# A two-layer hybrid encoder: the first gate placed in the opening's written order, queries transposed in float32 two heads at a time, and the splits behind the transposes given the heads' priority

## The chip, the cores and the metric

One core of one Trainium2 chip runs the whole program in one launch. The time is device microseconds (us) of an execution, and a version's time is the median of several executions. A core has five engines that run side by side, each with its own queue of instructions in a fixed order: TensorE (PE: matmuls and transposes, with weight loads shown apart as PEld), VectorE (DVE), ScalarE (ACT), GpSimd (POOL) and SyncE (SP, here the queue that starts the weight transfers). An engine stops at the head of its queue until the semaphores that this instruction waits for are set; everything queued behind it waits too.

## The reference

Two layers of an encoder over 256 tokens of width 1024, in float32. Each layer has a half-step SwiGLU network, a mixing stage of two attention branches on one joint projection, and a second SwiGLU network:

```python
for l in range(DEPTH):
    x = x + 0.5 * swiglu(rms_norm(x, ffn1_norm[l]), ffn1_w_gate[l], ffn1_w_up[l], ffn1_w_down[l])
    h = rms_norm(x, mix_norm[l])
    z = h @ w_in[l]
    qa, ka, va, qs, ks_, vs, zg = jnp.split(z, splits, axis=-1)
    # 8 heads of 64 for qa, ka, va and qs; 2 shared heads for ks_, vs; q and k RMS-normed per head
    o_na = neighbourhood_attention(qa, ka, va, na_rpb[l])
    o_sw = sliding_window_gqa(qs, ks_, vs, t5_bias, sw_sink[l])
    g = jax.nn.sigmoid((zg + b_gate[l]).astype(jnp.float32))
    merged = g[:, :, 0] * (o_na @ w_branch_na[l]) + g[:, :, 1] * (o_sw @ w_branch_sw[l])
    x = x + merged @ w_out[l]
    x = x + 0.5 * swiglu(rms_norm(x, ffn2_norm[l]), ffn2_w_gate[l], ffn2_w_up[l], ffn2_w_down[l])

def swiglu(x, w_gate, w_up, w_down):
    return (jax.nn.silu(x @ w_gate) * (x @ w_up)) @ w_down
```

## The kernel before

**Products in three parts.** Every float32 operand of a large product is split in two f32r numbers, a high part (ACT copies it, `split_to` at L184) and a low part (DVE subtracts, L185). A product is then three matmuls: high by high (L170), low weights by high data (L171), high weights by low data (L172). Weights come in pieces of 256 rows by 512 columns: a transfer on SP's queue into one of 4 buffers `raw` (L142), then two tiles `wh` and `wl` in a ring of 6. A piece's next transfer can start when the `wl` subtract that last read its `raw` buffer is done.

**Tokens** are two tiles of 128 (`T` = 2). `project(t, pieces, n)` makes 24 matmuls for a token tile and one chunk of 512 columns into one of two PSUM tiles `g`; the `g` tile is free again when what reads it is done.

**What sets the order.** PE's order is that of the program. Work that comes later is put off with `defer(lag, key, fn)`, the lag counted in units of projection time, and `tick` runs what is due. For the other engines a scheduler puts the instructions in an order by priorities; code under `high_priority(500)` (the wrapper `urgent`, before the change around the steps of an attention head: `front`, `turn`, `back`) is put ahead of other work of its time. In the opening the order of ACT and DVE is written out instead: `linked(engine, emit)` (L124) ties an instruction behind the last one that was linked on this engine, as long as the dictionary `chain` is not empty.

**The opening** (L225, first chunk of the first layer's network). It makes the norm of both token tiles in halves, and the first chunk's four pieces in between (`pieces`), with `steps(t, i)` the six matmuls of token tile `t` and piece `i` (L237). Then come `square(t, half)` (ACT's sums of squares, L217, with the statistics `ms` on DVE, L221 and L222, and `rsqrt` on POOL), and the loads and splits of the second chunk (`second`: four pieces), all on the written order. After `opening` returns, the loop of `ffn` emits for each token tile the gate: `sg` = Silu on ACT (L453) and `hh` on DVE (L454), which reads the other half of the same `g` tile.

**The mixing stage** (`mix`, L477) projects in the order Q0 Q1 K0 K1 q1 q0 and so on (Q and K are queries and keys of the sliding-window branch for token tiles 0 and 1, q and k those of the neighbourhood branch, a and g values and gates). `normed` makes the normed `qn` or `kn` of a token tile: `z` and `sq` on ACT, `hv` on DVE, `rs_y` on POOL, then the product on DVE (L489). `queries` then splits `qn` into `qs` (per head 64 columns high, 64 low), and its turn transposes the eight heads one by one, four to each PSUM tile `tp` (two buffers), with ACT copying each `tp` into `qT` or `sqT` (L504): a head's 64 high rows and 64 low rows stand on the 128 partitions. `keys` doubles `kn` on POOL (L511) and transposes it in float32 (L519); ACT makes the high part, DVE the low one (`skT` in the sliding-window branch, `kh` and `kl` in the other, L521 and L522). A score `sc` (L558) is two matmuls for a query tile, with the stacked queries against high and low keys; `S`, `pt`, `ph`, `pl` and `po` are the steps of softmax and the product with the values.

Of the kernel before, what the change touches and what calls it, by code (L numbers as in the profile page):

```python
# [11 lines left out]
F32 = mybir.dt.float32  # L12
F32R = mybir.dt.float32r
# [3 lines left out]
ALU = mybir.AluOpType  # L17
# [41 lines left out]
def hybrid_encoder(ctx, tc, x, w_gu1, w_d1, w_in, b_gate, qk_gain, rpb, sink, t5,  # L59
# [30 lines left out]
    ident_r = const.tile([P, P], F32R, name="ident_r")  # L90
    nc.vector.tensor_copy(ident_r, ident)
# [133 lines left out]
    def opening(w, l):  # L225
# [35 lines left out]
        second = [piece(i, 1) for i in range(2)]  # L261
        square(1, 0, idle)
        square(1, 1, idle)
        second += [piece(i, 1) for i in range(2, KD // 2)]
        chain.clear()
        for i in (1, 2, 3):
            for t in range(T):
                steps(t, i)
# [39 lines left out]
    def ffn(l, n, w_gu, w_d, after):  # L308
        with tc.tile_pool(name="ffn", bufs=1) as fp:
# [126 lines left out]

            waiting = []
            for c in range(NFC):
                first = n == 0 and c == 0
                if first:  # L440
# [8 lines left out]
                pair = act.tile([P, T, FC], F32, name="hh", tag="xg", bufs=2)  # L449
                for t in range(T):  # L450
                    ps = both[t] if first else project(t, pieces, 512)
                    sg = fp.tile([P, FC], F32, name="sg", tag="sg", bufs=2)
                    nc.scalar.activation(sg, ps[:, :FC], AF.Silu, scale=rstd[t])  # L453
                    nc.vector.scalar_tensor_tensor(pair[:, t], ps[:, FC:], rstd[t], sg, op0=ALU.mult, op1=ALU.mult)  # L454
                waiting.append((c, pair))
# [21 lines left out]
    def mix(l, n, after):  # L477
        with tc.tile_pool(name="mix", bufs=1) as mp:
# [12 lines left out]

            def queries(key, ps, t, qT):
                qn = act.tile([P, NH, DH], F32, name="qn", tag="xg", bufs=2)
                normed(ps, t, NH, qn)
                qs = mp.tile([P, NH, 2, DH], F32R, name="qs", tag="qk", bufs=2)
                split_to(qs[:, :, 0, :], qs[:, :, 1, :], qn)

                def turn():
                    for half in range(2):
                        tp = ps_tp.tile([P, 4, P], F32R, name="tp", tag="tp")  # L500
                        for j in range(4):
                            nc.tensor.transpose(tp[:, j, :], qs[:, 4 * half + j].rearrange("p two d -> p (two d)"),
                                                ident_r)
                        nc.scalar.activation(qT[:, 4 * half:4 * half + 4, t * P:(t + 1) * P], flipped(tp), AF.Copy)  # L504

                defer(QK_LAG + MORE.get(key, 0), key, turn)

            def keys(key, ps, t, nh, g, kh, kl):
# [4 lines left out]

                def turn():
# [16 lines left out]
            def attend(name, ins, qT, kh, kl, kidx, bias_of, vcol, ready, oT, sink_l=None):  # L531
# [5 lines left out]
                def urgent(fn):  # L537
                    def run(*args):
                        with tc.high_priority(500):
                            fn(*args)  # L540
                    return run

                @urgent
                def front(h):
# [11 lines left out]
                    for t in range(T):  # L556
                        for i, k in enumerate((kh, kl)):
                            nc.tensor.matmul(ps[:, t, :], qT[:, h, t * P:(t + 1) * P], k[:, kidx(h), :],  # L558
# [50 lines left out]
            sqT = mp.tile([P, NH, S], F32R, name="sqT", tag="sq")  # L609
            skT = pair("skT", "sk", [2, S])  # L610
            sv = mp.tile([P, T, 2, 3 * DH], F32R, name="sv")
            qT = mp.tile([P, NH, S], F32R, name="qT")
# [222 lines left out]
```

## Time and profile before

| | us |
|---|---|
| median of 3 executions | 1078.03 (1077.65 to 1078.95) |
| the profiled execution's own time | 1077.96 |
| its span in the trace | 1076.2 |
| PE, DVE, ACT, POOL busy | 1069.2, 875.9, 671.6, 116.9 |
| `wl` from `raw` (DVE L185), 336 times | 404.6 |
| `wh` from `raw` (ACT L184), 336 times | 346.7 |
| projections on PE (`g`, L170 to L172), 2928 matmuls | 1139.0 in overlapping spans |

An execution takes longer than its span in the trace by the 1.8 us around it. The granted TensorE clock is 1.0 throughout. Matmuls are pipelined: a 128x512 matmul is busy 0.39 us in its row, but the next one starts 0.23 us after it, so sums of PE's rows count the overlap twice. The mixing stage of the first layer lies at about 195 to 350 us, that of the second 532 us later.

### The profile page before, as it was taken

What the parts mean: (1) busy time and instruction counts of PE and PEld (TensorE: products, weight loads), DVE (VectorE), ACT (ScalarE), POOL (GpSimd) and SP (SyncE); (2) the same over time, 40 slices, a digit from 0 to 9 for tenths busy, and PEclk for the clock granted to TensorE, in tenths of its full rate; (3) what the DMA queues carried; (4) which work ended last, traced back from release to release, by engine and by line L of the source; (5) the groups of instructions that cost most, each with busy time, mean ns of one, the idle gap of its engine ahead of it and who ended that gap; (6) DMA issues with size and microseconds to landing.
All of it is one profiled execution on the core that took longest, in us unless ns stands there. A gap on an engine that the chain in (4) does not pass through costs nothing.

```text
span 1076.2 us, 14744 instructions
## 1 busy us (share of the span) xinstructions
PE 1069.2 (99%) x5125; PEld 890.2 (83%) x5125; DVE 875.9 (81%) x1337; ACT 671.6 (62%) x1014; POOL 116.9 (11%) x118
## 2 busy tenths in 40 slices
PE   9999999999999999999999999999999999999998
PEld 6888888888888888888878888888888888888887
DVE  5688898889886768879877888988898867778795
ACT  6565754788764556565465665557877646566562
POOL 1000030243520000000000000003534000000000
PEclk9999999999999999999999999999999999999999
DMA  8667665765654667756657766648666555776562
GB/s 259 214 217 237 211 206 176 227 199 151 195 184 137 202 201 241 244 167 193 208 160 232 235 210 206 183 150 242 181 196 180 181 173 161 236 232 204 197 196 78
DMA packets 98828, 212.63 MB, mean 198 GB/s; under 512 B 7569, under 2 KB 13745, under 8 KB 98753
## 3 DMA queue, kind: packets, MB, share of 16 engines
q1 hardware_dynamic: 98560, 211.60, 62.4%
q8 instruction: 40, 0.66, 0.2%
q14 instruction: 36, 0.29, 0.1%
q0 software_dynamic: 192, 0.08, 0.1%
HBM read 210.59 MB, written 1.06 MB: 197 GB/s over the span
## 4 chain that ended last, share of the span: by engine, by line
PE 95%; DVE 2%; ACT 1%; issue 1%; DMA 0%
PE g L170 22%; PE g L172 22%; PE g L171 22%; PE acc L170 5%; PE acc L172 5%; PE acc L171 5%; PE tp L318 2%; PE sc L558 1%; PE po L593 1%; PE tp L170 1%; PE tp L172 1%; PE pt L579 1%; PE tp L171 1%; DVE wl L185 1%; PE tp L201 1%
## 5 line engine op out<-in xcount | busy, mean ns | idle before, releaser
L185 DVE TENSOR_TENSOR wl<-raw,wh 128x1024 fp32r<-128x1024 f32 x336 | 404.6, 1217 | 67.8 <-ACT wh L184 65.2
L184 ACT ACTIVATE wh<-raw 128x1024 fp32r<-128x1024 f32 x336 | 346.7, 1045 | 129.4 <-DMA raw<-in_w_gu 47.8
L170 PE MATMUL g<-wh,xh 128*128 128x512 f32 (+1 forms) x976 | 383.8, 393 | 0.8 <-DVE hh L454 0.8
L172 PE MATMUL g<-wh,xl 128*128 128x512 f32 (+1 forms) x976 | 377.8, 387 | 0.7 <-DVE xl L185 0.7
L171 PE MATMUL g<-wl,xh 128*128 128x512 f32 (+1 forms) x976 | 377.4, 387 | 0.0
L172 PEld LDWEIGHTS g<-wh,xl 128*128 128x128 f32 x976 | 183.4, 188 | 40.0 <-DVE xl L185 2.1
L170 PEld LDWEIGHTS g<-wh,xh 128*128 128x128 f32 x976 | 183.6, 188 | 33.9 <-DVE hh L454 1.2
L171 PEld LDWEIGHTS g<-wl,xh 128*128 128x128 f32 x976 | 183.7, 188 | 32.7
L453 ACT ACTIVATE sg<-g,rs_y 128x256 f32<-128x256 f32 x88 | 41.0, 466 | 91.1 <-PE g L172 78.7
L454 DVE SCALAR_TENSOR_TENSOR hh<-g,rs_y,sg 128x256 f32<-128x256 f32 x88 | 42.1, 479 | 54.0 <-ACT sg L453 53.9
L170 PE MATMUL acc<-wh,hi 128*128 128x512 f32 x180 | 71.1, 395 | 0.0
L172 PE MATMUL acc<-wh,lo 128*128 128x512 f32 x180 | 70.2, 390 | 0.0
L171 PE MATMUL acc<-wl,hi 128*128 128x512 f32 x180 | 70.1, 389 | 0.0
L176 POOL TENSOR_TENSOR rs_y<-ms,mhalf 128x1 f32<-128x1 f32 x12 | 6.7, 554 | 553.5 <-DVE ms L222 545.1
L350 DVE TENSOR_TENSOR u<-raw 128x512 f32<-128x512 f32 x64 | 41.9, 685 | 15.2 <-DMA raw<-in_w_d 15.0
L184 ACT ACTIVATE corner<-raw 128x512 fp32r<-128x512 f32 x32 | 20.2, 631 | 50.1 <-DMA raw<-in_w_d 33.0
L571 POOL TENSOR_TENSOR S<-S,sm 128x512 f32<-128x512 f32 x32 | 37.1, 1160 | 65.7 <-DVE sm L570 38.3
L172 PEld LDWEIGHTS acc<-wh,lo 128*128 128x128 f32 x180 | 33.8, 188 | 7.2
L171 PEld LDWEIGHTS acc<-wl,hi 128*128 128x128 f32 x180 | 33.8, 188 | 6.8
L170 PEld LDWEIGHTS acc<-wh,hi 128*128 128x128 f32 x180 | 33.8, 188 | 6.7
L564 ACT ACTIVATE S<-S,mx 128x256 f32<-128x256 f32 x64 | 31.9, 500 | 8.0 <-DVE mx L561 7.9
L185 DVE TENSOR_TENSOR lo<-a,hi 128x896 fp32r<-128x896 f32 x32 | 33.8, 1084 | 0.5 <-ACT hi L184 0.5
(189 smaller groups left out, 1510.4 us busy)
## 6 DMA issues: line engine op xcount, KB each, us to landing
raw<-in_w_gu SPq DMA_DIRECT2D x176, 512.0 KB, 4.2
raw<-in_w_d SPq DMA_DIRECT2D x100, 512.0 KB, 4.0
raw<-in_w_in SPq DMA_DIRECT2D x64, 512.0 KB, 4.5
raw<-in_w_out SPq DMA_DIRECT2D x16, 512.0 KB, 3.6
bb<-in_b_gate SPq DMA_DIRECT2D x16, 256.0 KB, 3.6
raw<-in_w_bsw SPq DMA_DIRECT2D x8, 512.0 KB, 3.9
raw<-in_w_bna SPq DMA_DIRECT2D x8, 512.0 KB, 3.5
raw<-in_w_d SPq DMA_DIRECT2D x12, 256.0 KB, 2.6
```

The costliest lines, as they stand in the source:

```text
L170: nc.tensor.matmul(ps, xh, wh, start=first, stop=False)
L171: nc.tensor.matmul(ps, xh, wl, start=False, stop=False)
L172: nc.tensor.matmul(ps, xl, wh, start=False, stop=last)
L184: linked("act", lambda: nc.scalar.activation(hi, src, AF.Copy))
L185: linked("dve", lambda: nc.vector.tensor_tensor(lo, src, hi.bitcast(F32), ALU.subtract))
L201: nc.tensor.transpose(tp[:, i, :], xs[t][:, k * P:(k + 1) * P], ident)
L318: nc.tensor.transpose(tp[:, SLOT[t][i], :], hh[:, t, i * P:(i + 1) * P], ident)
L350: sub = lambda to, x, y: nc.vector.tensor_tensor(to, x, y, ALU.subtract)
L453: nc.scalar.activation(sg, ps[:, :FC], AF.Silu, scale=rstd[t])
L454: nc.vector.scalar_tensor_tensor(pair[:, t], ps[:, FC:], rstd[t], sg, op0=ALU.mult, op1=ALU.mult)
L564: nc.scalar.activation(S_[:, t, :], S_[:, t, :], AF.Exp, bias=mx[:, t:t + 1], scale=-1.0, accum_out=sm[:, t:t + 1])
L571: nc.gpsimd.tensor_tensor(S_, S_, sm.unsqueeze(2).to_broadcast([P, T, S]), ALU.mult)
```

## The change

Three edits go together.

**The opening.** The matmul steps of pieces 1 to 3 are written ahead of the second chunk's loads, and a new argument `early` emits token tile 0's gate between the third square and the second of the second chunk's pieces, with `linked`, so that it stands there in the written order. The gate itself becomes a function `glu(t, ps, pair)`. PE's order in the opening stays.

**The queries.** `qn` stays float32 and isn't split. Two heads stand side by side in 128 columns, so a token tile takes four float32 transposes into one `tp` tile (with `ident`; `ident_r` and its cast go). Behind the transposes, `split_to` runs twice on 64 partitions: for even heads (e = 0) and odd heads (e = 1), ACT writes the high part to the heads' own 64 partitions and DVE the low part to the other 64. `qT` and `sqT` get the parity as a dimension of its own, and the score matmuls index `qT[:, h % 2, h // 2]`. DVE's subtract waits for ACT's copy of the same parity, and ACT's second copy waits for DVE's first subtract; the `tp` tile is free after DVE's second.

**Priority.** `urgent` moves ahead of `queries` and `keys` and wraps their turns too.

```diff
@@ opening @@
-    def opening(w, l):
+    def opening(w, l, early):
...
-        second = [piece(i, 1) for i in range(2)]
+        for i in (1, 2, 3):
+            for t in range(T):
+                steps(t, i)
+        second = [piece(0, 1)]
         square(1, 0, idle)
+        early(ps[0])
+        second.append(piece(1, 1))
         square(1, 1, idle)
         second += [piece(i, 1) for i in range(2, KD // 2)]
         chain.clear()
-        for i in (1, 2, 3):
-            for t in range(T):
-                steps(t, i)
@@ ffn @@
+            def glu(t, ps, pair):
+                if t == 0:
+                    pair[0] = act.tile([P, T, FC], F32, name="hh", tag="xg", bufs=2)
+                sg = fp.tile([P, FC], F32, name="sg", tag="sg", bufs=2)
+                linked("act", lambda: nc.scalar.activation(sg, ps[:, :FC], AF.Silu, scale=rstd[t]))
+                linked("dve", lambda: nc.vector.scalar_tensor_tensor(pair[0][:, t], ps[:, FC:], rstd[t], sg,
+                                                                     op0=ALU.mult, op1=ALU.mult))
...
-                    both, second = opening(w_gu, l)
+                    both, second = opening(w_gu, l, lambda ps: glu(0, ps, pair))
...
                 for t in range(T):
-                    ps = both[t] if first else project(t, pieces, 512)
...
+                    if not first:
+                        glu(t, project(t, pieces, 512), pair)
+                    elif t:
+                        glu(t, both[t], pair)
@@ mix @@
             def queries(key, ps, t, qT):
-                qn = act.tile([P, NH, DH], F32, name="qn", tag="xg", bufs=2)
+                qn = mp.tile([P, 2, NH, DH], F32, name="qn", tag="qk", bufs=2)[:, 0]
                 normed(ps, t, NH, qn)
-                qs = mp.tile([P, NH, 2, DH], F32R, name="qs", tag="qk", bufs=2)
-                split_to(qs[:, :, 0, :], qs[:, :, 1, :], qn)
-
+
+                @urgent
                 def turn():
-                    for half in range(2):
-                        tp = ps_tp.tile([P, 4, P], F32R, name="tp", tag="tp")
-                        for j in range(4):
-                            nc.tensor.transpose(tp[:, j, :], qs[:, 4 * half + j].rearrange("p two d -> p (two d)"),
-                                                ident_r)
-                        nc.scalar.activation(qT[:, 4 * half:4 * half + 4, t * P:(t + 1) * P], flipped(tp), AF.Copy)
+                    tp = ps_tp.tile([P, 4, P], F32, name="tp", tag="tp")
+                    for j in range(4):
+                        nc.tensor.transpose(tp[:, j, :], qn[:, 2 * j:2 * j + 2].rearrange("p two d -> p (two d)"), ident)
+                    cols = slice(t * P, (t + 1) * P)
+                    for e in range(2):
+                        a, b = e * DH, (1 - e) * DH
+                        split_to(qT[a:a + DH, e, :, cols], qT[b:b + DH, e, :, cols], flipped(tp[a:a + DH]))
...
+                @urgent
                 def turn():
                     for h0 in range(0, nh, 4):
...
-                            nc.tensor.matmul(ps[:, t, :], qT[:, h, t * P:(t + 1) * P], k[:, kidx(h), :],
+                            nc.tensor.matmul(ps[:, t, :], qT[:, h % 2, h // 2, t * P:(t + 1) * P], k[:, kidx(h), :],
```

What the change moves is seen in the order of the instructions on each engine. First ACT in the opening, where `idle,ssq` are the squares (of token tile 0, then 1), `wh` the copies of the second and then the third chunk's pieces, and `sg` the gates of token tile 0 and 1. Before:

```order
L217 ACTIVATE idle,ssq<-x_80 128x512 x2
L184 ACTIVATE wh<-raw 128x1024 x2
L217 ACTIVATE idle,ssq<-x_81 128x512
L453 ACTIVATE sg<-g,rs_y 128x256
L217 ACTIVATE idle,ssq<-x_81 128x512
L184 ACTIVATE wh<-raw 128x1024 x2
L453 ACTIVATE sg<-g,rs_y 128x256
L184 ACTIVATE wh<-raw 128x1024 x2
```

With the change:

```order
L215 ACTIVATE idle,ssq<-x_80 128x512 x2
L182 ACTIVATE wh<-raw 128x1024
L215 ACTIVATE idle,ssq<-x_81 128x512
L441 ACTIVATE sg<-g,rs_y 128x256
L182 ACTIVATE wh<-raw 128x1024
L215 ACTIVATE idle,ssq<-x_81 128x512
L182 ACTIVATE wh<-raw 128x1024 x3
L441 ACTIVATE sg<-g,rs_y 128x256
```

The first `sg` passes one `wh`; the second `sg` now stands behind five `wh` and not four, the fifth being the third chunk's first piece.

Next DVE at the same place, with `hh` of token tiles 0 and 1, `ms` the statistics and `wl` the subtracts. Before:

```order
L221 TENSOR_TENSOR ms<-ssq 128x1
L222 TENSOR_SCALAR ms<-ms 128x1
L185 TENSOR_TENSOR wl<-raw,wh 128x1024 x2
L454 SCALAR_TENSOR_TENSOR hh<-g,rs_y,sg 128x256
L221 TENSOR_TENSOR ms<-ssq 128x1
L222 TENSOR_SCALAR ms<-ms 128x1
L185 TENSOR_TENSOR wl<-raw,wh 128x1024 x2
L454 SCALAR_TENSOR_TENSOR hh<-g,rs_y,sg 128x256
```

With the change:

```order
L219 TENSOR_TENSOR ms<-ssq 128x1
L220 TENSOR_SCALAR ms<-ms 128x1
L183 TENSOR_TENSOR wl<-raw,wh 128x1024
L442 SCALAR_TENSOR_TENSOR hh<-g,rs_y,sg 128x256
L183 TENSOR_TENSOR wl<-raw,wh 128x1024
L219 TENSOR_TENSOR ms<-ssq 128x1
L220 TENSOR_SCALAR ms<-ms 128x1
L183 TENSOR_TENSOR wl<-raw,wh 128x1024 x3
L442 SCALAR_TENSOR_TENSOR hh<-g,rs_y,sg 128x256
```

The first `hh` passes one `wl`; the second stands behind one `wl` more, again that of the third chunk's first piece.

Last DVE in the first layer's mixing stage, between the second query tile and the first score of the sliding-window branch. `skT` are the low halves of the two key tiles, `qn` the normed queries of the neighbourhood branch, `sqT` the new subtracts. Before:

```order
L185 TENSOR_TENSOR wl<-raw,wh 128x1024 x2
L489 TENSOR_TENSOR qn<-z,rs_y 128x512
L522 SCALAR_TENSOR_TENSOR skT<-tp,qkg,skT 128x2x128
L185 TENSOR_TENSOR wl<-raw,wh 128x1024 x2
L522 SCALAR_TENSOR_TENSOR skT<-tp,qkg,skT 128x2x128
L185 TENSOR_TENSOR qs<-qn,qs 128x8x64
L486 TENSOR_REDUCE hv<-sq 128x8
```

With the change:

```order
L183 TENSOR_TENSOR wl<-raw,wh 128x1024
L183 TENSOR_TENSOR sqT<-tp,sqT 64x4x128
L183 TENSOR_TENSOR wl<-raw,wh 128x1024
L537 SCALAR_TENSOR_TENSOR skT<-tp,qkg,skT 128x2x128
L497 TENSOR_TENSOR qn<-z,rs_y 128x512
L183 TENSOR_TENSOR wl<-raw,wh 128x1024
L183 TENSOR_TENSOR sqT<-tp,sqT 64x4x128
L183 TENSOR_TENSOR wl<-raw,wh 128x1024
L537 SCALAR_TENSOR_TENSOR skT<-tp,qkg,skT 128x2x128
L494 TENSOR_REDUCE hv<-sq 128x8
```

Two subtracts of the second query tile come in ahead of the key tiles' low halves, the first `skT` passes `qn`, and the `qs` subtract behind the second is gone. On PE nothing moves but the transposes: `MATMUL tp<-ident_r,qs 128x128 x8` becomes `MATMUL tp<-ident,qn 128x128 x4` at eight places. The transposes of the second sliding-window key tile now use the `tp` buffer of the first, and so wait for its `skT`.

More of the change, by code (lines that the diff above doesn't have):

```diff
@@ L89, in hybrid_encoder @@
     make_identity(nc, ident)
-    ident_r = const.tile([P, P], F32R, name="ident_r")
-    nc.vector.tensor_copy(ident_r, ident)
     mhalf = const.tile([P, 8], F32, name="mhalf")
@@ L439, in ffn @@
                 first = n == 0 and c == 0
+                pair = [None]
                 if first:
[L441 removed]
+                    both, second = opening(w_gu, l, lambda ps: glu(0, ps, pair))
                 elif n == 0 and c == 1:
@@ L448, in ffn @@
                     prepare(prep[c])
-                pair = act.tile([P, T, FC], F32, name="hh", tag="xg", bufs=2)
                 for t in range(T):
-                    ps = both[t] if first else project(t, pieces, 512)
[L452 to L455, printed above, removed]
+                    if not first:
+                        glu(t, project(t, pieces, 512), pair)
+                    elif t:
+                        glu(t, both[t], pair)
+                waiting.append((c, pair[0]))
                 if c % 2 or c >= NFC - 3:
@@ L490, in normed, with urgent, run @@
                                         r.unsqueeze(2).to_broadcast([P, nh, DH]), ALU.mult)
+            def urgent(fn):
+                def run(*args):
+                    with tc.high_priority(500):
+                        fn(*args)
+                return run
             def queries(key, ps, t, qT):
-                qn = act.tile([P, NH, DH], F32, name="qn", tag="xg", bufs=2)
+                qn = mp.tile([P, 2, NH, DH], F32, name="qn", tag="qk", bufs=2)[:, 0]
                 normed(ps, t, NH, qn)
-                qs = mp.tile([P, NH, 2, DH], F32R, name="qs", tag="qk", bufs=2)
-                split_to(qs[:, :, 0, :], qs[:, :, 1, :], qn)
+                @urgent
                 def turn():
-                    for half in range(2):
-                        tp = ps_tp.tile([P, 4, P], F32R, name="tp", tag="tp")
-                        for j in range(4):
-                            nc.tensor.transpose(tp[:, j, :], qs[:, 4 * half + j].rearrange("p two d -> p (two d)"),
-                                                ident_r)
-                        nc.scalar.activation(qT[:, 4 * half:4 * half + 4, t * P:(t + 1) * P], flipped(tp), AF.Copy)
+                    tp = ps_tp.tile([P, 4, P], F32, name="tp", tag="tp")
[5 more added lines that the diff above has]
+                        split_to(qT[a:a + DH, e, :, cols], qT[b:b + DH, e, :, cols], flipped(tp[a:a + DH]))
                 defer(QK_LAG + MORE.get(key, 0), key, turn)
@@ L535, in attend @@
                     bias = [bias_of(0), bias_of(1)]
[L537 to L541, printed above, removed]
                 @urgent
@@ L607, in pair @@
                 return both[:, 0], both[:, 1]
-            sqT = mp.tile([P, NH, S], F32R, name="sqT", tag="sq")
+            sqT = mp.tile([P, 2, NH // 2, S], F32R, name="sqT", tag="sq")
             skT = pair("skT", "sk", [2, S])
             sv = mp.tile([P, T, 2, 3 * DH], F32R, name="sv")
-            qT = mp.tile([P, NH, S], F32R, name="qT")
+            qT = mp.tile([P, 2, NH // 2, S], F32R, name="qT")
             kT = (mp.tile([P, NH, S], F32R, name="kh", tag="kh"), mp.tile([P, NH, S], F32R, name="kl"))
```

## The prediction

> **What bounds the kernel now.** I read the busy times first, then the chain that ended last, then what TensorE (PE) waited for in all.
>
> ```profile
> PE 1069.2 (99%) x5125; PEld 890.2 (83%) x5125; DVE 875.9 (81%) x1337; ACT 671.6 (62%) x1014; POOL 116.9 (11%) x118
> PE 95%; DVE 2%; ACT 1%; issue 1%; DMA 0%
> PE idle L120 <- DVE blank L115: 1.6, 1, 1.6
> PE g L170 <- DVE hh L454: 0.8, 1, 0.8
> PE g L172 <- DVE xl L185: 0.7, 1, 0.7
> ```
>
> PE is busy for 99% of the span and holds 95% of the chain. The last three rows are all the waits the trace names for it (total, times, longest): 3.1 us in 1076, 0.8 of them behind `hh` in the opening. So only two things shorten this kernel: PE issuing less, or that wait going. Work taken from VectorE (DVE) or ScalarE (ACT) is worth nothing, and work added there costs only where it makes PE late. The profiled execution took 1077.96 us (span 1076.2 and 1.8 around it), 0.07 under the median of 1078.03; the sum is made against it. A measurement of this kernel tells about 0.2% (2.2 us) from no change: faster is under 1075.9, slower over 1080.2.
>
> **Part 1, fewer transposes.** A token tile of queries now takes eight f32r transposes (L502); it will take four float32 ones. The trace has a batch of four with the same kind of operand, `pt` (L579).
>
> ```profile
> L502 PE MATMUL tp<-ident_r,qs 128*128 128x128 f32 x64 | 6.4, 244 | 0.0
> 208.59 0.80 PE L502 MATMUL tp<-ident_r,qs 128*128 128x128 f32 x8
> 209.22 0.46 PE L170 MATMUL g<-wh,xh 128*128 128x512 f32 x1
> 209.52 0.39 PE L171 MATMUL g<-wl,xh 128*128 128x512 f32 x1
> 233.44 0.60 PE L579 MATMUL pt<-ident,S 128*128 128x128 f32 x4
> 233.79 0.48 PE L170 MATMUL g<-wh,xh 128*128 128x512 f32 x1
> 234.10 0.40 PE L171 MATMUL g<-wl,xh 128*128 128x512 f32 x1
> ```
>
> Matmuls overlap, so a batch costs the distance between starts, not its busy time. Eight: 208.59 to 209.22 is 0.63, and the matmul behind needs 0.30 to the next. Four: 0.35, then 0.31. That is 0.93 against 0.66, 0.27 saved per batch. 64 transposes are 8 batches (two token tiles, two attention branches, two layers): **8 x 0.27 = 2.2 us**, 1.1 in each layer's attention stage. PE's other rows are unchanged.
>
> A rule would turn this term round: a float32 pass through PE as four passes. The f32r batch steps by 0.63 / 8 = 0.08; four times four of these are 1.27, so a batch would lose 0.64 and the eight 5.1 us. The row at 233.44 speaks against it: four float32 transposes stepped by 0.35, 0.09 each. The Trainium skill, "FP8 and Floating Point Precision", TensorE Precision Notes, says that true FP32 takes four passes through the PE array; for transposes the 0.09 of this trace decides. It stays a rival, nearly without a chance.
>
> **Part 2, the splits behind the transposes.** `qs` goes: one ACT copy and one DVE subtract per tile. The tile's two ACT copies from PSUM stay, with 64 partitions; two DVE subtracts from PSUM come.
>
> ```profile
> L185 DVE TENSOR_TENSOR lo<-tp,hi 128x512 fp32r<-128x512 f32 x12 | 8.2, 682 | 0.1
> L185 DVE TENSOR_TENSOR qs<-qn,qs 128x512 fp32r<-128x512 f32 x8 | 5.5, 682 | 0.0
> L184 ACT ACTIVATE qs<-qn 128x512 fp32r<-128x512 f32 x8 | 5.0, 622 | 0.0
> ```
>
> The trace has no 64-partition split of 512 columns; the nearest is `lo` out of PSUM at 0.68. So ACT loses 8 x 0.62 = 5.0 us and DVE gains 8 x (2 x 0.68 - 0.68) = 5.5 us, 2.7 per layer. Whether that reaches PE is a matter of place. The tightest is the first score of the sliding-window branch, which needs the second key tile's low half `skT`.
>
> ```profile
> 219.52 1.23 DVE L185 TENSOR_TENSOR wl<-raw,wh 128x1024 fp32r<-128x1024 f32 x1 [0.87 <-ACT wh L184]
> 221.26 0.48 DVE L522 SCALAR_TENSOR_TENSOR skT<-tp,qkg,skT 128x256 fp32r<-128x256 f32 x1
> 223.09 1.23 DVE L185 TENSOR_TENSOR wl<-raw,wh 128x1024 fp32r<-128x1024 f32 x1 [0.22 <-ACT wh L184]
> 224.24 0.48 DVE L522 SCALAR_TENSOR_TENSOR skT<-tp,qkg,skT 128x256 fp32r<-128x256 f32 x1
> 224.88 0.64 PE L558 MATMUL sc<-skT,sqT 128*128 128x256 f32 x4
> ```
>
> `skT` ends at 224.72. The first score's matmul for the low half, the second of four that start 0.12 apart, is due at 225.00. Two batches lie ahead, so PE arrives 0.54 earlier, at 224.46. Two new subtracts come ahead of `skT`, some 1.2 us in a queue where starts overlap by a little; the idle 0.87 and 0.22 take 1.09 of it. With no other shift `skT` ends at 224.72 + 1.2 - 1.1 = 224.8; with everything before it 0.3 earlier, as PE's projections are, at 224.5. The stall is 0.0 to 0.4, and after a wait PE needs another 0.1. One step ahead, K1's transposes will take the PSUM bank that K0's `skT` frees, due at 220.7 and freed about then (221.26 + 0.48, less 0.6 for the `qn` it now passes, plus 0.6 for a subtract, less the idle 0.87, is 220.9): 0 to 0.5, but a stall here uses up the one at the score. I take **0.2 per stage, 0.4 in all** (0 to 1.2), nearer the low end, because both come out within 0.3 of just fitting.
>
> Behind this place DVE has room until its first full stretch:
>
> ```profile
> 205.00:225.00 20.00, 20.00 (x117) 17.25 (x115) 17.17 (x28) 17.32 (x29) 7.60 (x8) 1.00 0.74 220
> 225.00:242.00 17.00, 17.00 (x98) 14.47 (x96) 14.32 (x34) 14.32 (x32) 8.97 (x6) 1.00 0.68 211
> 241.70 0.41 DVE L598 TENSOR_TENSOR o<-o,po 64x256 f32<-64x256 f32 x1 [0.91 <-ACT o L597]
> 242.35 0.69 DVE L185 TENSOR_TENSOR pl<-pt,ph 128x512 fp32r<-128x512 f32 x1 [0.24 <-ACT ph L184]
> 257.31 0.48 DVE L529 SCALAR_TENSOR_TENSOR va<-g,rs_y,va 128x256 fp32r<-128x256 f32 x1
> 258.20 0.39 PE L170 MATMUL g<-wh,xh 128*128 128x512 f32 x1
> ```
>
> The windows' third busy figure is DVE's: 17.17 of 20 and 14.32 of 17 us, so 5.5 us idle against 2.7 added. All four query batches lie ahead of 236, and the idle 0.91 and 0.24 just before 242.4 show that DVE there waits for others. I take nothing for the stretch behind.
>
> **Part 3, the opening.** `sg` and `hh` of token tile 0 move ahead. Rows of PE, ACT and DVE:
>
> ```profile
> 18.47 0.61 PE L237 MATMUL g<-wl,xh 128*128 128x512 f32 x2
> 19.83 0.61 PE L237 MATMUL g<-wl,xh 128*128 128x512 f32 x2
> 21.21 0.50 PE L170 MATMUL g<-wh,xh 128*128 128x512 f32 x1 [0.77 <-DVE hh L454]
> 21.55 0.40 PE L171 MATMUL g<-wl,xh 128*128 128x512 f32 x1
> 24.29 0.39 PE L171 MATMUL g<-wl,xh 128*128 128x512 f32 x1
> 26.78 0.39 PE L170 MATMUL g<-wh,xh 128*128 128x512 f32 x1
> 17.32 1.99 ACT L184 ACTIVATE wh<-raw 128x1024 fp32r<-128x1024 f32 x2
> 19.83 0.46 ACT L453 ACTIVATE sg<-g,rs_y 128x256 f32<-128x256 f32 x1
> 23.95 1.06 ACT L184 ACTIVATE wh<-raw 128x1024 fp32r<-128x1024 f32 x1 [0.79 <-DMA raw<-in_w_gu]
> 18.40 2.36 DVE L185 TENSOR_TENSOR wl<-raw,wh 128x1024 fp32r<-128x1024 f32 x2 [0.60 <-ACT wh L184]
> 20.68 0.48 DVE L454 SCALAR_TENSOR_TENSOR hh<-g,rs_y,sg 128x256 f32<-128x256 f32 x1
> 21.88 2.36 DVE L185 TENSOR_TENSOR wl<-raw,wh 128x1024 fp32r<-128x1024 f32 x2 [0.47 <-ACT wh L184]
> 24.16 0.47 DVE L454 SCALAR_TENSOR_TENSOR hh<-g,rs_y,sg 128x256 f32<-128x256 f32 x1
> ```
>
> Tile 0's sums end at 18.47 + 0.61 = 19.08. PE could go on at 20.28 (19.83 plus two steps of 0.23) but starts at 21.21, and its first step after the wait is 0.34 (to 21.55) in place of 0.23: **1.04 us lost**. `hh` at 20.68 stood behind `sg` (19.83) and two `wl`. After: ACT does one `wh` (to 18.4), one square, then `sg` at 19.10 to 19.57; DVE's first `wl` ends at 19.6, `hh` runs 19.6 to 20.1. PE is not stalled there.
>
> What is late next is what `hh` passed. The second `wh` follows at 19.5 to 20.5, its `wl` ends at 21.8 (PE needs it at about 21.9, so it fits); two short statistics rows; third `wl` 22.1 to 23.3, which PE needs at 24.29 - 1.04 = 23.25. A stall of 0.1 to 0.2 and the 0.1 restart: 0.26. Then tile 1's `hh`, at 24.16 now: it comes to stand behind the split of the third chunk's first weights, whose copy could only start at 23.95, when its DMA had landed. PE needs that `hh` at 26.78 - 1.04 + 0.26 = 26.0. If the transfer lands as before, ACT has `wh` to 25.0 and `sg` to 25.4, DVE `wl` to 26.2, `hh` to 26.6: a stall of 0.6, 0.7 with the restart, so nearly all is given back. But the next transfer on SyncE's queue waits for the `wl` that is now a us later, so this one shares the memory with less; the fastest in this stretch took 3.6 us:
>
> ```profile
> DMA to landing us min/median/max: 3.6/5.2/6.2
> ```
>
> Issued when the first `wl` has freed its buffer (19.6), it would land at 23.25 and `hh` end at 26.0, a stall of 0.2. Gain: 1.04 - 0.26 - (0.2 to 0.7), 0.6 to 0.1. I take **0.6**, with 0 and 1.04 as ends, since the moved issue does favour this transfer. The dropped `ident_r` copy ran beside the first loads and is worth nothing.
>
> **The sum:** 1077.96 - 2.2 + 0.4 - 0.6 = **1075.6**.
>
> **Rivals.** (a) The opening gives all back and the attention stages stall for 0.3 to 0.6 each: 1077.96 - 2.2 + 0.8 = 1076.6 (down to 1076.0). For it: `hh` really stands behind a DMA wait now. (b) The new chain copy, subtract, copy, subtract per tile holds PSUM banks and DVE longer, and each batch's saving returns as waits at K1's transposes and the first score: with 1.1 lost per stage, 1077.4. For it: the two places fit only to within 0.3. (c) No stall appears: 1077.96 - 2.2 - 1.04 = 1074.7. (d) **Slower:** DVE's full stretch from 242.4 to 258 starts late. PE at 258.20 waits for `va` that ends at 257.79, 0.41 to spare. A DVE lag of x us there moves PE by x - 0.41 in each layer, whatever PE saved ahead; with all 2.7 us unabsorbed each layer loses 2.3, with the opening's 0.6: 1077.96 + 4.6 - 0.6 = 1082.0. It decides for slower than before from x = 0.7, beyond the 0.2% from x = 1.8. Against it: 5.5 us idle ahead. (e) Float32 transposes at four passes: 1077.96 + 5.1 - 0.6 = 1082.5.
>
> **How the numbers follow.** Forecast (1075.1 to 1076.0) 0.44, of which 0.08 lies above 1075.9; (a) 0.20; (b) 0.13; (c) 0.13; (d) 0.09; (e) 0.01. Faster: 0.36 + 0.13 = 0.49. Same: 0.08 + 0.20 + 0.13 = 0.41. Slower: 0.10. The range goes from (c) to just above (b), 1074.5 to 1077.7, and leaves out (d), (e) and a little at both ends. Faster alone holds 1074.5 to 1075.9.
>
> **What would show it.** In the new trace: batches of four L514 transposes stepping by 0.35 (0.6 would be rule (e)); PE with no gap at 20.3; small gaps at 23.2 and 26.0, and whether the third chunk's first `wh` starts at 23.3 or 23.9; gaps at K1's transposes (220.7) or the first score (224.5); `va` near 257 in DVE's stretch. The prediction is wrong if PE's waits gain more than 1 us anywhere else, above all behind 242.

## The result, and the profile after

| | before | with the change |
|---|---|---|
| median, us | 1078.03 (1077.65 to 1079.31) | 1081.57 (1080.53 to 1082.49) |
| executions | 7 | 7 |
| the profiled execution, us | 1077.96 | 1080.64 |
| its span, us | 1076.2 | 1078.9 |

The change makes the kernel slower by 0.3%: the ratio is 1.003, with an interval of 1.002 to 1.004. The forecast was 1075.6 us with 1074.5 to 1077.7 around it. The profiled execution is near the low end of its kind; its 2.7 us over before are what the trace can explain.

The page of the changed kernel, first its busy times and the engines of the chain that ended last, then all that TensorE (PE) waited for (in total, times, longest; in us):

```profile
PE 1069.4 (99%) x5093; PEld 887.7 (82%) x5093; DVE 883.9 (82%) x1344; ACT 667.7 (62%) x1006; POOL 122.2 (11%) x118
PE 92%; DVE 5%; issue 1%; ACT 1%; POOL 0%; POOLq 0%; DVEq 0%; ACTq 0%
PE idle L118 <- DVE blank L113: 1.6, 1, 1.6
PE tp L534 <- DVE qT L183: 1.1, 2, 0.6
PE pt L588 <- POOL S L580: 1.1, 2, 0.7
PE tp L534 <- DVE skT L537: 1.0, 2, 0.5
PE g L170 <- DVE xl L183: 0.7, 1, 0.7
PE sc L567 <- DVE skT L537: 0.3, 2, 0.2
```

The 0.8 us behind `hh` is gone, and four waits have come in its place, each twice, once per layer: 3.5 us. VectorE's (DVE) share of the chain rose from 2% to 5%. Each wait costs more than its row, since the matmuls behind it start late as well (as at 21.21 to 21.55 before).

Because PE's instructions stand in the same order, the start of each can be compared between the two traces. The change is 0.40 us ahead at 100 us, 0.56 at 200; at 300 us it is 1.18 behind; at 720 us 1.27, at 840 us 2.71. So the opening gained 0.39, the first attention stage lost 1.75 and the second 1.44, and the stretches between moved by less than 0.2 each. The steps in the first stage, with their rows (at a row's end the idle time before it and what ended it):

```profile
208.02 0.60 PE L514 MATMUL tp<-ident,qn 128*128 128x128 f32 x4
208.38 0.49 PE L168 MATMUL g<-wh,xh 128*128 128x512 f32 x1
208.70 0.39 PE L169 MATMUL g<-wl,xh 128*128 128x512 f32 x1
...
220.78 0.41 PE L534 MATMUL tp<-ident,kn 128*128 128x128 f32 x2 [0.51 <-DVE skT L537]
224.92 0.62 PE L567 MATMUL sc<-skT,sqT 128*128 128x256 f32 x3 [0.17 <-DVE skT L537]
242.86 0.63 PE L534 MATMUL tp<-ident,kn 128*128 128x128 f32 x4 [0.56 <-DVE qT L183]
254.54 0.66 PE L588 MATMUL pt<-ident,S 128*128 128x128 f32 x4 [0.74 <-POOL S L580]
```

A batch of four float32 transposes steps by 0.36, then 0.32; against before each batch puts PE ahead by 0.25 to 0.29, four by 1.1 us. The four stalls, with what follows each, take 0.66 (second key tile's transposes), 0.43 (first score), 0.73 (neighbourhood keys' transposes) and 0.96 (softmax transposes), 2.8 in all. Less the 1.1 this is 1.7 of the stage's 1.75. In the second layer the same four take 0.66, 0.43, 0.75 and 0.58, which is 1.3 of 1.44.

VectorE's queue ahead of the first two; the first row is from the kernel before, the others are from the change:

```profile
216.35 0.69 DVE L486 TENSOR_REDUCE hv<-sq 128x8 f32<-128x512 f32 x1 [1.01 <-ACT sq L484]
...
216.03 0.29 DVE L497 TENSOR_TENSOR kn<-z,rs_y 128x128 f32<-128x128 f32 x1 [0.98 <-PE tp L514]
216.24 0.68 DVE L494 TENSOR_REDUCE hv<-sq 128x8 f32<-128x512 f32 x1
...
218.29 0.69 DVE L183 TENSOR_TENSOR sqT<-tp,sqT 64x512 fp32r<-64x512 f32 x1
219.01 1.23 DVE L183 TENSOR_TENSOR wl<-raw,wh 128x1024 fp32r<-128x1024 f32 x1
220.15 0.48 DVE L537 SCALAR_TENSOR_TENSOR skT<-tp,qkg,skT 128x256 fp32r<-128x256 f32 x1
...
222.39 0.69 DVE L183 TENSOR_TENSOR sqT<-tp,sqT 64x512 fp32r<-64x512 f32 x1
224.38 0.48 DVE L537 SCALAR_TENSOR_TENSOR skT<-tp,qkg,skT 128x256 fp32r<-128x256 f32 x1
```

`kn` waits 0.98 us at the head of the queue for the transposes that read its buffer, and `hv`, which waits for nothing of them, stands behind. (In the kernel before `hv` stood ahead of this `kn`.) From 216.03 to 225.4 VectorE has no gap over 0.05 us, so each of the two `sqT` subtracts puts off the key tiles' `skT`, for which PE waits.

The third and fourth stall in the change:

```profile
240.31 0.69 DVE L183 TENSOR_TENSOR qT<-tp,qT 64x512 fp32r<-64x512 f32 x1
242.02 0.69 DVE L183 TENSOR_TENSOR qT<-tp,qT 64x512 fp32r<-64x512 f32 x1
...
244.09 1.67 DVE L497 TENSOR_TENSOR kn<-z,rs_y 128x512 f32<-128x512 f32 x1
...
248.21 2.37 DVE L183 TENSOR_TENSOR wl<-raw,wh 128x1024 fp32r<-128x1024 f32 x2
...
251.31 0.15 DVE L578 TENSOR_TENSOR sm<-sm,es 128x2 f32<-128x2 f32 x1
251.39 0.68 DVE L183 TENSOR_TENSOR pl<-pt,ph 128x512 fp32r<-128x512 f32 x1
251.99 1.21 DVE L183 TENSOR_TENSOR wl<-raw,wh 128x1024 fp32r<-128x1024 f32 x1
253.12 0.15 DVE L579 RECIPROCAL sm<-sm 128x2 f32<-128x2 f32 x1
253.44 1.04 POOL L580 TENSOR_TENSOR S<-S,sm 128x512 f32<-128x512 f32 x1 [5.08 <-ACT va L543]
```

The same reciprocal, the product that needs it and the transposes of that product in the kernel before:

```profile
248.51 0.16 DVE L570 RECIPROCAL sm<-sm 128x2 f32<-128x2 f32 x1
248.85 1.04 POOL L571 TENSOR_TENSOR S<-S,sm 128x512 f32<-128x512 f32 x1 [2.24 <-PE g L172]
253.39 0.60 PE L579 MATMUL pt<-ident,S 128*128 128x128 f32 x4
```

The fourth query tile's transposes ran at 234.3, but its second subtract ends at 242.7, and only then is the PSUM buffer free that the keys' transposes at 242.86 take. The softmax transposes at 254.54 wait for GpSimd's (POOL) product, which needs the reciprocal at 253.12: a 0.15 us instruction behind two `wl`, a `pl` and another `wl`.

The fourth stall is more than a queue that runs late. In the kernel before the reciprocal stood ahead of the second of those `wl`, of `pl` and of the last `wl`, and its product was done at 249.89, 3.5 us before PE took it. The scheduler has written VectorE's order anew at this place, which the list of moved instructions ahead of the prediction leaves out. All runs below bear this out, in both layers: the change, `e2_queries`, `e3_copies`, `e5_half`, `e6_half_copies` and `e14_no_subtract` have the new order, and there the product ends 0.05 us before the transposes, so that any lag of VectorE or ScalarE reaches PE; the other ten kernels have the reciprocal in its old place, and there it ends at least 1.97 us before. The size of the wait differs between the layers as `kn` (at 244.09) does: `kn` takes 1.67 us in the first and 1.33 in the second, where it took 1.04 before, and PE's wait is 0.74 and 0.36. Why `kn` takes longer is not shown; GpSimd works beside it (`b` from 244.02).

### The profile page after: what moved, and what is told of

It reads as the page before. It is cut to its first block, busy times and chain, and to the rows that moved or that the text cites. A ratio compares the mean times of both kernels' runs of the same rounds, so it can differ in the third digit from the quotient of the medians.

```text
span 1078.9 us, 14671 instructions
## 1 busy us (share of the span) xinstructions
PE 1069.4 (99%) x5093; PEld 887.7 (82%) x5093; DVE 883.9 (82%) x1344; ACT 667.7 (62%) x1006; POOL 122.2 (11%) x118
## 4 chain that ended last, share of the span: by engine, by line
PE 92%; DVE 5%; issue 1%; ACT 1%; POOL 0%; POOLq 0%; DVEq 0%; ACTq 0%
PE g L170 21%; PE g L168 21%; PE g L169 21%; PE acc L168 5%; PE acc L170 5%; PE acc L169 5%; DVE wl L183 2%; PE tp L318 2%; PE tp L168 1%; PE tp L170 1%; PE tp L169 1%; PE po L602 1%; PE sc L567 1%; PE pt L588 1%; PE g L235 1%
## 5 line engine op out<-in xcount | busy, mean ns | idle before, releaser
L580 POOL TENSOR_TENSOR S<-S,sm 128x512 f32<-128x512 f32 x32 | 39.7, 1241 | 61.0 <-DVE sm L579 31.1
```

Of the source, the lines that this page charges most:

```text
L580: nc.gpsimd.tensor_tensor(S_, S_, sm.unsqueeze(2).to_broadcast([P, T, S]), ALU.mult)
```

## The experiments

In the expectations, theory A is that VectorE's added work makes PE late, B that the chain copy, subtract, copy, subtract holds a buffer, C another reason, D that the place of the split behind the transposes does it. One thing needs no run: built with `urgent` taken off the two turns, the program has the instructions of all five engines in the same order as the change. The third edit moves nothing.

The medians are beside the runs of the kernel before on the same chip (1078.0 to 1078.3). "Opening", "layer 1" and "layer 2" are PE's shift against the trace of before (plus is later) as worked out above, at 16 to 100, 200 to 300 and 720 to 840 us. They come from one execution each, which in `e10_q0` took 1.0 us more than the median, in `e5_half` 0.8 less, in the change 0.9 less. In the stretches between, which no edit touches, the shift moved by -0.4 to +0.6 us (100 to 200) and by up to +1.0 (300 to 720), and the two layers of one run, which have the same code, differ by up to 0.45 (`e7_double` by more). So differences of a few tenths between two rows tell little.

| run | median us | ratio, interval | opening | layer 1 | layer 2 |
|---|---|---|---|---|---|
| the change | 1081.57 | 1.003 [1.002, 1.004] | -0.39 | +1.75 | +1.44 |
| e1_opening | 1077.94 | 0.9997 [0.9988, 1.0006] | -0.49 | 0.01 | 0.11 |
| e2_queries | 1081.80 | 1.0033 [1.0021, 1.0045] | 0.01 | +1.76 | +1.71 |
| e3_copies | 1081.32 | 1.0029 [1.0018, 1.0041] | +0.32 | +1.64 | +1.63 |
| e5_half | 1079.93 | 1.0020 [1.0012, 1.0029] | -0.47 | +0.88 | +1.09 |
| e6_half_copies | 1080.52 | 1.0023 [1.0014, 1.0032] | +0.23 | +1.18 | +1.15 |
| e7_double | 1084.07 | 1.0050 [1.0037, 1.0063] | 0.01 | +1.99 | +3.77 |
| e8_mixed | 1079.32 | 1.0009 [1.0000, 1.0018] | -0.67 | +1.09 | +0.83 |
| e9_gates | 1077.60 | 0.9994 [0.9985, 1.0003] | -0.67 | -0.01 | 0.03 |
| e10_q0 | 1077.42 | 0.9993 [0.9984, 1.0002] | -0.66 | 0.00 | +0.21 |
| e12_early5 | 1080.43 | 1.0019 [1.0010, 1.0028] | -0.16 | +1.17 | +0.83 |
| e11_early3 | 1079.28 | 1.0008 [0.9999, 1.0017] | -0.67 | +1.02 | +0.66 |
| e11_early5 | 1081.93 | 1.0034 [1.0021, 1.0046] | -0.66 | +2.08 | +2.53 |
| e13_half_transposes | 1076.92 | 0.9988 [0.9979, 0.9996] | 0.05 | -0.65 | -0.49 |
| e14_no_subtract | 1078.84 | 1.0006 [0.9997, 1.0015] | -0.48 | +0.49 | +0.26 |

### The two halves of the change

`e1_opening` has the edits of `opening` and `ffn` alone, `e2_queries` those of `mix` (and `ident_r`) alone.

> The kernel before with the opening's edits alone. Common reading of the two traces: after 27 us the changed kernel's TensorE is 0.42 us ahead (0.55 by 145 us), so this should give 1077.5 to 1077.6, a gain of 0.4 to 0.6, and the wait behind hh gone with three small gaps near 22.3 to 26.6 in its place. Rival: the shifted transfers of the first chunks cost as much later: 1078.0 or more.

> The change without the opening's edits. If the loss lies in the attention stages and the parts do not interact: 1081.57 + 0.5 = 1082.1, with the same four stalls per layer (second key tile's transposes, first score, transposes of the neighbourhood keys, the softmax transposes behind GpSimd's product). Rival: the opening shifts the phase between TensorE and VectorE and makes the stalls: 1078 or less.

The opening gains 0.49 in the trace, 0.2 in the medians, which is no more than the runs scatter. The queries alone lose what the whole change loses. The parts do not interact, and the loss is in the attention stages.

### The chain, VectorE's work, both

`e3_copies` writes both copies ahead of both subtracts:

```diff
+                    lo = []
                     for e in range(2):
...
-                        split_to(qT[a:a + DH, e, :, cols], qT[b:b + DH, e, :, cols], flipped(tp[a:a + DH]))
+                        hi, src = qT[a:a + DH, e, :, cols], flipped(tp[a:a + DH])
+                        nc.scalar.activation(hi, src, AF.Copy)
+                        lo.append((qT[b:b + DH, e, :, cols], src, hi.bitcast(F32)))
+                    for args in lo:
+                        nc.vector.tensor_tensor(*args, ALU.subtract)
```

> The change with both ScalarE copies of a query tile written ahead of both VectorE subtracts, so that the second copy waits for no subtract. The same work on each engine. Theory B (the chain copy, subtract, copy, subtract holds the transposes' PSUM buffer and spreads the subtracts): the stalls at the neighbourhood keys' transposes (0.75 each) and behind them at the softmax transposes (0.9 and 0.5) go, 1081.57 - 2.9 = 1078.7. Theory A (VectorE has 0.7 us more work per tile in a stretch where TensorE waits for it): the stalls move but their sum stays, 1081 to 1082.

`e5_half` keeps that chain and leaves out half of each subtract, with a ScalarE copy in its place; `e6_half_copies` also writes the copies first. The edit of `e5_half`:

```diff
-                        split_to(qT[a:a + DH, e, :, cols], qT[b:b + DH, e, :, cols], flipped(tp[a:a + DH]))
+                        hi, lo, src = qT[a:a + DH, e, :, cols], qT[b:b + DH, e, :, cols], flipped(tp[a:a + DH])
+                        nc.scalar.activation(hi, src, AF.Copy)
+                        nc.scalar.activation(lo[:, 2:], src[:, 2:], AF.Copy)
+                        nc.vector.tensor_tensor(lo[:, :2], src[:, :2], hi.bitcast(F32)[:, :2], ALU.subtract)
```

> The change with each of the two subtracts cut to half its heads (64x256 in place of 64x512, some 0.4 us in place of 0.7); for heads 4 to 7 ScalarE writes a copy of the high values where the low halves belong, 64x256 each. The chain of four steps per tile stays. So VectorE has about its work of before, ScalarE too. Theory A: the stalls at the first score and at the softmax transposes go almost wholly and the time is 1078 or less, down to 1077. Theory B: all four stalls stay, 1081 to 1082, as the chain is one step longer on ScalarE.

> Both: the subtracts cut to half their heads (for heads 4 to 7 the low halves are copies of the high values) and both high copies ahead of both subtracts. VectorE has about its work of before and no step waits for another engine twice. If VectorE's added work and the chain are the whole loss, the four stalls per layer go and the full saving of the eight batches shows: 1078.1 - 2.3 - 0.4 = 1075.4, with no stall over 0.2 in the attention stages. Rival C (the transposes' data arrive late for another reason, such as GpSimd's order or the reuse of the PSUM buffer by the second key tile): 0.5 to 1.0 per layer stays, 1076.5 to 1077.5.

With the chain cut, both keys' transposes wait no longer, but the softmax transposes wait for more, 3.0 us in place of 1.1 (first of PE's waits in `e3_copies`):

```profile
PE pt L593 <- POOL S L585: 3.0, 4, 1.1
```

The loss per layer stays at 1.64. So B names two places, not the loss. Half the subtracts take 0.9 and 0.35 off a layer's loss, not all of it, and with the chain cut as well 0.6 and 0.3; by the medians, 1079.93 and 1080.52, the two runs can't be told apart. Both lie outside what either theory expected of them. Neither A alone nor B alone holds: something else is left, of some 2 us per layer (about 1.1 of net loss, and the 1.1 of the batches that does not show). Part of it is the order: both runs have the reciprocal in its new place, and in `e5_half` `qn` also stands ahead of the first `skT` again, and PE's wait for that `skT` is 0.9 in place of 0.5.

### The same work ahead of the transposes

`e7_double` is the kernel before with the `qs` subtract written twice.

```diff
                 split_to(qs[:, :, 0, :], qs[:, :, 1, :], qn)
+                nc.vector.tensor_tensor(qs[:, :, 1, :], qn, qs[:, :, 0, :].bitcast(F32), ALU.subtract)
```

> The kernel before with the qs subtract of each query tile done twice on VectorE: 0.68 us more per tile, 5.5 us in all, as in the change, but no new chain, no other transposes and no other layout. Theory A (VectorE's work alone makes TensorE late): TensorE stalls at the first score or the softmax transposes, 0.5 to 1.2 per layer, 1079 to 1080.5. Theory B or C (chain, buffers or order): VectorE's idle time takes it, 1078.0 to 1078.4.

```profile
235.46 0.68 DVE L489 TENSOR_TENSOR kn<-z,rs_y 128x512 f32<-128x512 f32 x1
236.06 0.68 DVE L497 TENSOR_TENSOR qs<-qn,qs 128x512 fp32r<-128x512 f32 x1
...
236.89 0.85 PE L503 MATMUL tp<-ident_r,qs 128*128 128x128 f32 x8 [1.75 <-DVE qs L497]
```

Three of the four extra subtracts of a layer cost nothing. The fourth was put behind a `wl` and a `kn` in VectorE's queue, and PE waits 1.75 us for it, at a place that nobody named; 1084.07 lies above both expectations. The second layer's 3.77 has the same wait and then 1.5 us lost to matmuls at half the clock, of which the last section tells. An extra 0.68 us costs by where it lands, from nothing to more than twice its length.

### The opening's second gate, and fewer tiles

`e9_gates` ties token tile 1's gate ahead of the third chunk's first split. `e8_mixed` adds float32 transposes for Q0 and q1, `e10_q0` for Q0 alone (the keys named are those of `queries`).

```diff
         second += [piece(i, 1) for i in range(2, KD // 2)]
+        early(ps[1], 1)
+        gates_done.update(chain)
         chain.clear()
...
+                    if n == 0 and c == 2:
+                        chain.update(gates_done)
                     pieces = columns(w_gu, l, c * 512, 512)
+                    chain.clear()
...
+                packed = key in ("Q0", "q1")
```

> The kernel before with the opening's edits and the gate of token tile 1 tied ahead of the third chunk's first split. The gap at the start of the second chunk's token tile 1 (0.26, with a late transfer 0.9) goes; that at the third weights (0.26) stays: a gain of 0.7 to 0.8 in the opening, 1077.3. If that gap came from the transfers rather than from the order on VectorE and ScalarE: 1077.9 as with the opening's edits alone.

> The gates as in the run before this, and float32 transposes only for the first sliding-window and the first neighbourhood query tile of each layer (Q0 and q1), with both copies ahead of both subtracts; the other two tiles as in the kernel before. VectorE's added work is halved and lies where it has idle time behind it. If the stalls come from the added work between the second query tile and the first score and around the neighbourhood keys, the four batches keep 0.29 each and the stalls nearly go: 1078.1 - 0.8 - 1.2 + 0.4 = 1076.5. If any new subtract costs its own length: 1078 to 1080.

> The gates as in e9_gates, and the float32 transposes with both copies first for the first sliding-window query tile (Q0) of each layer alone; the other three tiles as before. In the mixed run TensorE gained 0.4 at Q0 in the first layer with no stall up to the first score, and stalled only behind q1. So two batches keep 0.3 to 0.4 each: 1078.2 - 0.6 - 0.7 = 1076.9, below both kernels. Rival (a subtract behind the transposes always comes back as a stall somewhere): 1077.6 or more.

The gate's order gives 0.67 in the opening, near the 0.7 to 0.8 expected; the median is 0.6 under before, the interval reaches 1.0003. Two tiles lose 1.09 and 0.83 where four lose 1.75 and 1.44, and one tile gives 0.00 and +0.21: in the profiled execution what a single batch saves, about 0.3, is returned before the stages end. (That execution took 1078.41, against the median of 1077.42, the second longest of 11.) `e8_mixed` missed its 1076.5 and `e10_q0` its 1076.9. Both `e9_gates` and `e10_q0` have a median below both kernels, but neither can be told from the kernel before.

### Earlier transposes

```diff
-                defer(QK_LAG + MORE.get(key, 0), key, turn)
+                defer(QK_LAG - 5 + MORE.get(key, 0), key, turn)
```

> The change with one number altered: the query tiles' transposes come due 5 units (3.4 us of projections) earlier; nothing else is edited. Theory D (the split now starts only behind the transposes, and so its copies and subtracts fall between the keys' norms and the first scores, where VectorE's queue is late for TensorE; with earlier transposes they have back the room that the qs split had): the stalls at both keys' transposes go and those at the softmax transposes shrink, 1078 to 1079. Theory A (VectorE's 0.7 us per tile in that stretch decides, wherever it is put): 1080.5 to 1081.6.

> All four query tiles in float32 with both copies first, transposes 3 units (2.0 us) earlier, and the gates of e9_gates. Theory D: most of the 2.3 us of saved transposes shows and at most 1 us of stalls is left per layer, 1076 to 1077.5. Theory A: as e3_copies less the 0.6 of the gates, 1080.5.

> As the run before this with the transposes 5 units (3.4 us) earlier. Theory D: better than with 3 units or equal, 1075.5 to 1077. Theory A: 1080.5. If the earlier transposes wait for qn (its ready time is 4 to 6 us ahead of the transposes in the kernel before): new waits of TensorE on qn, up to 1 us per layer.

The waits at the keys' transposes and at the first score are gone from PE's list in `e12_early5` and `e11_early3`. A new one comes at 258 us, where the values' low half `va` is due, in each layer; in `e11_early3`:

```profile
257.20 0.39 PE L173 MATMUL g<-wh,xl 128*128 128x512 f32 x1
258.68 0.47 PE L171 MATMUL g<-wh,xh 128*128 128x512 f32 x1 [1.09 <-DVE va L569]
```

This is the place of the prediction's rival (d). `e12_early5` has it too (2.2 us in all), and in `e11_early5` the softmax transposes wait 3.7 us in its stead. A lag that is taken away at one place comes out at the next. Theory D missed in all three: `e12_early5` took 1080.4 where D said 1078 to 1079 and A 1080.5 to 1081.6, and the other two took 1079.3 and 1081.9 where D said 1076 to 1077.5 and 1075.5 to 1077.

### PE's saving alone, and the split without VectorE

`e13_half_transposes` leaves the split ahead of the transposes and halves the transposes. `e14_no_subtract` is the change with ScalarE copies for the low halves.

```diff
-                    for half in range(2):
-                        tp = ps_tp.tile([P, 4, P], F32R, name="tp", tag="tp")
-                        for j in range(4):
-                            nc.tensor.transpose(tp[:, j, :], qs[:, 4 * half + j].rearrange("p two d -> p (two d)"),
-                                                ident_r)
+                    tp = ps_tp.tile([P, 4, P], F32R, name="tp", tag="tp")
+                    for j in range(4):
+                        nc.tensor.transpose(tp[:, j, :], qs[:, j].rearrange("p two d -> p (two d)"), ident_r)
+                    for half in range(2):
```

```diff
-                        split_to(qT[a:a + DH, e, :, cols], qT[b:b + DH, e, :, cols], flipped(tp[a:a + DH]))
+                        src = flipped(tp[a:a + DH])
+                        nc.scalar.activation(qT[a:a + DH, e, :, cols], src, AF.Copy)
+                        nc.scalar.activation(qT[b:b + DH, e, :, cols], src, AF.Copy)
```

> The kernel before with half of the query transposes left out: heads 4 to 7 of each query tile get copies of what heads 0 to 3 have. The split ahead of the transposes, VectorE's and ScalarE's work stay; TensorE issues four f32r transposes per tile in place of eight (from the row of eight, 4 x 0.08 = 0.3 us less each). If the saving on TensorE is worth its length as long as the other engines do nothing more (the first term of the prediction): 1078.2 - 2.5 = 1075.7. If VectorE already sets the pace in this stretch: stalls take it back, 1077.3 to 1078.2.

> The change with no VectorE subtract behind the transposes: the low halves are ScalarE copies of the high values. VectorE then has 0.68 us less per query tile than before, ScalarE 0.6 more than before and 1.2 more than in the change. If VectorE's work behind the transposes is the loss: no stall over 0.2 is left in the attention stages and the four batches' saving shows, 1075.5 to 1076. If it is the place of the split behind the transposes, whichever engine does it: stalls at the keys' transposes and the softmax transposes stay, 1079 to 1081.

The two rows are a wait of PE in each run, `e13_half_transposes` first:

```profile
PE pt L578 <- POOL S L570: 0.5, 3, 0.2
```

```profile
PE sc L569 <- DVE skT L539: 0.9, 2, 0.4
```

With nothing added anywhere, a batch saves 0.3 to 0.35 and a stage 1.4 us, of which it keeps 0.65 and 0.49; the rest goes again at the softmax transposes, the `va` place and a product behind it, with 0.1 to 0.3 at each. The expectation of 1075.7 missed by 1.2, and the measured 1076.9 lies short of the other one's 1077.3. So more than half of such a saving does not show even with the other engines' work as it was. With the split behind the transposes but no subtract there, a stage loses 0.49 and 0.26, though VectorE has 2.7 us less to do than before: four ScalarE copies in a row hold up the `wh` copies behind them (ScalarE has no idle time from 214.5 to 224), and VectorE's `wl` and `skT` come later in turn. VectorE also stood 1.53 us at `qn` there for GpSimd's `rs_y`, so this reading of the wait is argued, not shown. The median of 1078.84 is far from the 1075.5 to 1076 of the first theory and just under the 1079 to 1081 of the second. ScalarE in the first stage of `e14_no_subtract`:

```profile
216.80 0.58 ACT L519 ACTIVATE sqT<-tp 64x512 fp32r<-64x512 f32 x1
217.39 0.59 ACT L520 ACTIVATE sqT<-tp 64x512 fp32r<-64x512 f32 x1
218.00 0.59 ACT L519 ACTIVATE sqT<-tp 64x512 fp32r<-64x512 f32 x1
218.60 0.59 ACT L520 ACTIVATE sqT<-tp 64x512 fp32r<-64x512 f32 x1
219.10 1.05 ACT L182 ACTIVATE wh<-raw 128x1024 fp32r<-128x1024 f32 x1
```

Of the first stage's swing this gives two parts, each a difference of two rows of the table: from -0.65 (the saving as it can show) to +0.49 when the split moves behind the transposes, 1.1 us; from +0.49 to +1.75 when VectorE does the low halves, 1.3 us. In the second stage 0.75 and 1.2. The parts are not clean: the first has the reciprocal's new place in it, `e14_no_subtract` gives ScalarE 1.2 us more per tile than the change, and the batches of `e13_half_transposes` save 0.3 to 0.35 in place of 0.27.

## Why the prediction was wrong

**What bounds the kernel: half right.** "PE is busy for 99%" holds for both kernels, and it led to the error. It says that PE seldom waits, not by how much the others are ahead. In the attention stages they are ahead by some tenths, and a PE that is 1.4 us quicker overtakes them (`e13_half_transposes`).

**Part 1: the size was right, its worth was not.** A batch saved 0.25 to 0.29 where 0.27 was forecast, and four float32 transposes stepped by 0.36 where 0.35 was: rival (e) was nothing. But "8 x 0.27 = 2.2 us" entered the sum whole, where `e13_half_transposes` keeps 1.1 of its 2.8 with the rest unchanged.

**Part 2 is the step that failed.** It found the two places (K1's transposes and the first score) and took 0.2 per stage; they cost 1.09. Its line "the idle 0.87 and 0.22 take 1.09 of it" came true, for the queue there has no idle left. But it took "everything before it 0.3 earlier". In the change `kn` with its 0.98 us wait stands ahead of `hv`, and `hv` starts at 216.24: 0.45 later than in the kernel before, once the 0.56 us by which the whole kernel is ahead at 200 us is taken off. And the two subtracts take 1.45 us of the queue (218.29 to 219.01, 222.39 to 223.12) where 1.2 was forecast. Then "5.5 us idle against 2.7 added" and "I take nothing for the stretch behind" are wrong by 1.69 us in the first layer and 1.33 in the second: the chain holds a buffer until 242.7, and the reciprocal lost its 3.5 us of room. The sum took VectorE's order as it was, with the new work added. The windows of the change (the third busy figure is VectorE's):

```profile
205.00:225.00 20.00, 19.33 (x104) 16.04 (x102) 18.19 (x30) 16.05 (x25) 8.74 (x8) 1.00 0.72 216
225.00:242.00 17.00, 17.00 (x91) 14.38 (x92) 15.16 (x34) 13.18 (x29) 8.47 (x5) 1.00 0.62 179
```

VectorE is still idle for 1.8 + 1.8 = 3.6 us of these 37, and PE waits for it at two places in them. Idle time in a queue with a fixed order is there because the instruction at its head waits for another engine; work that stands behind that head cannot use it. Room has to be read as the slack of each instruction that PE waits for, not as idle time summed up.

**Part 3: right places, a range too narrow.** 0.6 was forecast for the opening; the trace of the change shows 0.39, that of `e1_opening` 0.49. The stalls are at the two places named, 0.26 and 0.26. How much is given back hangs on the third chunk's first transfer, as argued: its `wh` starts at 23.48 in the change, but at 24.17 in `e3_copies`, where it waited for the transfer and where the stall at `hh` takes 0.9 and the opening loses 0.3. Such a loss lay outside the ends of 0 and 1.04.

**The rivals.** (d) had the direction and the engine: slower, by VectorE's lag. That its 1082.0 comes so near the 1081.57 measured is luck: it put 2.3 us per layer on a lag at `va`, and in the change PE does not wait for `va` at all, as four earlier waits take the lag first; at `va` itself it shows in `e11_early3` and `e12_early5`. It got 0.09 because of the 5.5 us. (b) had the first two places and their size (1.1 forecast, 1.09 measured); it stopped there, and the buffer that its chain holds costs at the third place, which it did not name. (a), the opening giving all back, is what `e3_copies` and `e6_half_copies` show.

What stays open: how the loss divides between ScalarE's and VectorE's queue, and how much of it would be left with the order of before. Every edit also changes the order that the scheduler writes, and no run held that order fixed.

## What to carry to other kernels

Where the other engines are ahead of the bound one by only tenths of a microsecond, most of a saving on it can be lost (here 1.1 of 2.8 us was kept); how far they are ahead is read as the slack of each thing it waits for, in the stage of the saving. Where a scheduler writes the order, compare the new order at each of these things: a 0.15 us reciprocal lost 3.5 us of slack by its new place. A step that is moved from ahead of a transpose to behind it falls from slack (here the `qs` subtracts of the first layer ended 1.4 to 2.1 us before PE's transposes) into the chain to the next consumer, and its buffers are held as long. Idle time of an in-order engine is room only for work that can be put ahead of the wait.

## What the runs showed of the hardware

A subtract or copy on 64 partitions took as long as on 128: VectorE 0.69 us for 64x512 against 0.68 for 128x512, ScalarE 0.59 in both forms. Two rows of the change, then ScalarE's 128-partition copy in the kernel before:

```profile
L183 DVE TENSOR_TENSOR sqT<-tp,sqT 64x512 fp32r<-64x512 f32 x8 | 5.5, 689 | 0.5
L182 ACT ACTIVATE qT<-tp 64x512 fp32r<-64x512 f32 x8 | 4.7, 587 | 0.2
L504 ACT ACTIVATE qT<-tp 128x512 fp32r<-128x512 f32 x8 | 4.3, 590 | 0.0
```

In `e7_double` the 1.74 us wait in the second layer was followed by a lower clock, the first layer's wait of 1.75 was not. The windows (the third figure from the end is the granted clock):

```profile
768.00:771.00 3.00, 1.44 (x9) 0.87 (x7) 3.00 (x8) 3.00 (x9) 1.21 (x2) 1.00 0.78 215
771.00:773.00 2.00, 1.82 (x11) 1.65 (x12) 2.00 (x4) 2.00 (x4) 0.51 (x1) 0.78 0.92 244
773.00:775.00 2.00, 2.00 (x6) 1.57 (x5) 2.00 (x4) 0.37 (x1) 0.39 (x1) 0.50 0.71 174
```

Matmuls that stepped by 0.23 stepped by 0.43 until about 775 us, which cost 1.5 us on top of the wait itself. The Trainium skill, "TensorE: Matmul & The Clock Gate", Part 1, puts the idle time after which the clock halves at about 3.4 us; here a wait of half that was followed by it once, and once not.
